# The second norm's weight and shift moved from token rows to the experts' transposed rows, and the first weight splits moved behind the first gather

## The chip, the core and the metric

The kernel runs on one core of a Trainium2 chip. The metric is the device time of one execution in microseconds (us); a lower time is better. The core has a matrix engine (PE, with PEld for its weight loads), a vector engine (DVE), an activation engine (ACT), GpSimd (POOL in the rows) and SyncE (SP), which issues most DMAs. Each takes its own instructions in order and waits for others by semaphores.

## What is computed

A whole model over 1024 tokens of width 1024 in float32: a first block of two attention layers, and a second block of a Fourier and window attention mix with a mixture of experts. The change concerns the end of the second block:

```python
h2 = rmsnorm(x, norm_ffn_g[l]) * (1.0 + sc2) + sh2
x = x + g2 * expert_choice_moe(h2, w_router[l], w_gate[l], w_up[l], w_down[l])

def expert_choice_moe(h, w_router, w_gate, w_up, w_down):
    cap = CAPACITY_FACTOR * S // N_EXPERTS          # 128 tokens
    aff = jax.nn.softmax(jnp.einsum('bsd,de->bse', h, w_router).astype(jnp.float32), axis=-1)
    g, idx = lax.top_k(aff.transpose(0, 2, 1), cap)
    xin = jax.vmap(lambda hb, ib: hb[ib])(h, idx)
    a = jnp.einsum('becd,edf->becf', xin, w_gate)
    u = jnp.einsum('becd,edf->becf', xin, w_up)
    y = jnp.einsum('becf,efd->becd', jax.nn.silu(a) * u, w_down)
    y = y * g[..., None].astype(y.dtype)
    ...
```

Here `sc2`, `sh2` and `g2` are three of the six parts of `mod`, a product of the conditioning vector with `w_ada`. The 16 experts each take the 128 tokens with the highest affinity, and their results, weighted, are added onto the rows of `x`.

## The kernel before

**Tiles and precision.** Tokens are worked in 8 tiles of 128 rows. A float32 product is made of three PE products of a high and a low half (`_h`, `_l`): ACT casts a tile to its high half, DVE subtracts that from the tile to get the low half (`kk.split`, lines 134 and 135), and lines 139 to 141 multiply high by high, low by high and high by low.

**The modulation vector.** Early in the program six rows of `mod` are made in pieces of 1x256 on one partition (lines 1297 to 1303) and written to memory as `mod_d`. Its row 3 holds weight times (1 + scale) of the second norm, row 4 its shift, row 5 the gate `g2`.

**The second norm (`norm2`, lines 2007 to 2044), once per tile, called by `out_phase` as the tiles of the second block's output projection come out.** PE transposes the tile, ACT and DVE split it, and PE makes 16 products with the router's weights, into which the weight of the norm is already multiplied (`wg`); the shift enters as a row sum `sw`. ACT reads the logits `rlg`, PE transposes them back (`prt`, line 2021), and the softmax follows in small instructions: `rz`, `rmx`, `rnm` on DVE, the exponential `rex` on ACT with its sum read by an accumulator instruction, then `rrc` (line 2032), `aff` (line 2033) and a spread copy `rep` (line 2050) on DVE, which PE transposes as `pa` (line 2052) so that ACT and DVE can keep it as `affr` and `affb`. The inverse root of the mean square, `r`, is made by ACT's sum of squares (`sqj`) and Newton steps on DVE over 128x1 (lines 148 to 163: `rsv`, `rsy`, `rsq`). Beside this the normed row `h2` is made in spare weight buffers (named `mraw`): for the first six tiles DVE multiplies `x` by `r` and by the broadcast weight `gB` in one instruction (line 2042); for the last two ACT multiplies by `r` (line 2039) and GpSimd by `gB` (line 2040); for all eight GpSimd adds the broadcast shift `sB` (line 2043). SP writes it to `h_d` (line 2044).

**The experts (`moe`, line 1619).** At its start the gate row is broadcast to `g2b` and halved by DVE (line 1624). Then 192 weight loads of 1 MB are issued by SP as buffers come free (line 1649; `mraw` and `xraw` are these buffers). Three quarters of each weight matrix are split, half a load at a time, into a ring of five slots, `ring_h` by ACT (line 1664) and `ring_l` by DVE (line 1665); the first five of these low halves are given to GpSimd (`spare`), behind the last `affr` copy. One quarter of the matrix is multiplied unsplit (line 1792). A threshold search of ten rounds follows (lines 1680 to 1688): a compare with a count over 128x1024 on DVE, `mok`, a PE product, and two small DVE instructions. Then come prefix counts and slots, and for each expert one-hot rows `oh`, a PE product `psel`, the row list `idx` and the gate (lines 1752 to 1759), and GpSimd's gather of 128 rows from `h_d` into `xg` (line 1756).

**The gathered rows.** `transposed(x, xT, g)` is called twice per expert for its rows: PE transposes four blocks of 128 columns into a PSUM tile `ptx`. For g = 0 ACT and DVE split blocks 2 and 3 (`xT_h`, `xT_l`), and ACT copies blocks 0 and 1 whole to `xTf` (line 1776), the operand of the unsplit products; for g = 1 all four blocks are split. The same function serves the hidden activations.

**What sets the order.** Up to the experts a scheduler places the recorded instructions on each engine by its own costs; `moe` itself, from its step functions on, is in the order in which it is written (`manual_schedule`): the first expert's one-hots, gather and transposes, then for each expert the products of gate, up and down, into whose parts the next expert's gather and transposes are put (parts 6 and 7 of the down product).

Of the kernel before, what the change touches and what calls it, by code (L numbers as in the profile page):

```python
# [11 lines left out]
F32 = mybir.dt.float32  # L12
# [1249 lines left out]
def ada_rows(kk, ps, a, mod_d):  # L1262
# [28 lines left out]
    def total(s, z, dst, gname, ap_):  # L1291
# [7 lines left out]
        nc.vector.tensor_tensor(x[0:1, :], pm[0:1, :H], b, op=ALU.add)  # L1299
        if gname:  # L1300
            nc.sync.dma_start(b, a[gname][:, z * H:z * H + H])
            nc.vector.scalar_tensor_tensor(x[0:1, :], x[0:1, :], 1.0, b, op0=ALU.add, op1=ALU.mult)
# [297 lines left out]
def moe_consts(kk, pool, a):  # L1600
# [3 lines left out]
    src = {"grp": a["c_grp"], "jsh": a["c_jsh"], "tri": a["c_tri"], "pidx": a["c_pidx"], "iota": a["c_iota"].to_broadcast([P, P])}  # L1604
    for nme, n, dt in (("grp", P, F32), ("jsh", 11, I32), ("tri", P, F16), ("pidx", 2 * NT, F32), ("iota", P, F16), ("one", P, F16)):
        c[nme] = pool.tile([P, n], dt, name="mc_" + nme)
# [9 lines left out]
def moe(kk, ctx, ax, a, con, aff, h2_d, acc_d, mod_d, raws, after):  # L1616

    nc = kk.nc
# [5 lines left out]
    nc.vector.tensor_scalar(g2, g2, 0.5, None, op0=ALU.mult)  # L1624
# [35 lines left out]
    def split_ahead(n, spare=False):  # L1660
        while count["split"] < min(n, len(splits)):
# [3 lines left out]
            (nc.gpsimd if spare else nc.vector).tensor_tensor(w.lo, raw_of(i), w.hi.bitcast(F32), op=ALU.subtract)  # L1665
# [4 lines left out]
    with kk.tc.issue_after(con["last"]):  # L1670
        split_ahead(RING, True)
# [97 lines left out]
    def transposed(x, xT, g):  # L1769

        pt = ps.tile([P, 4, P], F32, name=kk.nm("ptx"), **ptag)
        for j in range(4):
            nc.tensor.transpose(pt[:, j, :], x[:, (4 * g + j) * P:(4 * g + j + 1) * P], kk.ident)
        if g == 0:
            kk.split(xT.hl[:, 0:2, :], pt[:, 2:4])
            nc.scalar.copy(xT.full, pt[:, 0:2])
# [35 lines left out]
    def x_part(e, g):  # L1812
        if e < NE:
            if g == 0:
                xT[e] = Operand("xT")
            transposed(sel[e][2], xT[e], g)

    step_one_hots(0)
    step_gather(0)
    for g in range(2):  # L1820
        x_part(0, g)
# [27 lines left out]
def tile_model(ctx: ExitStack, tc: tile.TileContext, a: dict, out: bass.AP, part=None):  # L1849
# [116 lines left out]
    with kk.pool(name="c2", bufs=1) as op:  # L1966
        def setup():


            g2 = bcast(kk, op, mod_d[3:4, :], D, "gB3")  # L1970
            s2 = bcast(kk, op, mod_d[4:5, :], D, "sB3")
# [3 lines left out]
            cols = op.tile([P, 2, NK], F32, name="gscol")  # L1975
# [13 lines left out]
            return g2, s2, wr, sw, fold  # L1989
# [17 lines left out]
        def norm2(t, x):  # L2007
            if t == 0:
                router.extend(setup())
            g2, s2, wr, sw, fold = router  # L2010
# [27 lines left out]
            if t > 5:  # L2038
                nc.scalar.activation(h2, x, AF.Copy, scale=r)
                nc.gpsimd.tensor_tensor(h2, h2, g2, op=ALU.mult)  # L2040
            else:
                nc.vector.scalar_tensor_tensor(h2, x, r, g2, op0=ALU.mult, op1=ALU.mult)
            nc.gpsimd.tensor_tensor(h2, h2, s2, op=ALU.add)
# [105 lines left out]
```

## Time and profile before

| | |
|---|---|
| time, median of 3 runs (lowest to highest) | 2636.35 us (2634.61 to 2644.07) |
| profiled execution: time, span | 2629.75 us, 2628.0 us |
| busy: PE, DVE, ACT, POOL | 2338.4, 1841.4, 1265.6, 510.7 us |
| share of the span: PE, DVE, ACT, POOL | 89%, 70%, 48%, 19% |
| chain that ended last: PE, DMA, DVE, POOL, ACT | 56%, 17%, 12%, 5%, 3% |
| moved by DMA | 527.98 MB, 201 GB/s in the mean |

The span is the stretch from the first to the last instruction that the profiler saw; the execution's own time is a little longer. Matmul ends are modelled, so a busy PE is not necessarily at its peak. A row of the timeline gives the start, the duration, the engine, the line of the kernel, what it writes and reads with the shapes, and in brackets the idle time of that engine before it and what ended that.

### The profile page before, as it was taken

The numbers are of one execution on the slowest core, as the hardware profiler recorded it, in microseconds if no ns is written. First come the engines' busy times: TensorE is split into PE (matmuls) and PEld (weight loads), VectorE is DVE, ScalarE is ACT, GpSimd is POOL, SyncE is SP. The second block draws the span as 40 slices with busy tenths as digits, with TensorE's granted clock in tenths as the row PEclk, the third lists the DMA queues.
The fourth block names the chain that finished last, engine by engine and source line by source line (L and its number), as shares of the span: only waits on it lengthen the run. The fifth ranks groups of instructions, "written<-read, shape, count | busy, mean of one in ns | idle before, by whom it ended". The sixth has DMA issues, their size and how long they took to land.

```text
span 2628.0 us, 40820 instructions
## 1 busy us (share of the span) xinstructions
PE 2338.4 (89%) x14412; PEld 1844.6 (70%) x14412; DVE 1841.4 (70%) x4592; ACT 1265.6 (48%) x2423; POOL 510.7 (19%) x661
## 2 busy tenths in 40 slices
PE   7988978787978878899989969989974999999998
PEld 7866756665867866788767758877863776777676
DVE  4459989787866355366776576777676777777775
ACT  4344575465643243255654343355332555555554
POOL 0000027577770013100000031011022101110110
PEclk9999988897999899999999989999986999999999
DMA  4443376855656226854765452544564999999993
GB/s 129 134 124 100 113 206 167 208 162 183 185 167 205 77 98 255 255 145 124 191 186 157 135 195 68 140 119 157 197 264 168 359 369 357 356 374 367 356 357 128
DMA packets 298653, 527.98 MB, mean 201 GB/s; under 512 B 44086, under 2 KB 187598, under 8 KB 298448
## 3 DMA queue, kind: packets, MB, share of 16 engines
q1 hardware_dynamic: 282320, 467.69, 54.5%
q0 software_dynamic: 16128, 57.68, 6.9%
q8 instruction: 114, 1.87, 0.3%
q14 instruction: 91, 0.75, 0.1%
HBM read 409.37 MB, written 115.65 MB: 200 GB/s over the span
## 4 chain that ended last, share of the span: by engine, by line
PE 56%; DMA 17%; DVE 12%; POOL 5%; issue 5%; ACT 3%; SPq 2%; POOLq 0%; DVEq 0%; ACTq 0%
PE sb L139 6%; PE sb L140 6%; PE sb L141 6%; PE sb L288 4%; DMA adw<-w_ada 4%; PE ptp L335 3%; DVE tkj L392 3%; PE w_gate L1792 2%; POOL adw L1283 2%; PE w_up L1792 2%; PE w_down L1792 2%; PE w_gate L139 2%; PE w_gate L141 2%; PE w_gate L140 2%; PE w_up L139 2%
## 5 line engine op out<-in xcount | busy, mean ns | idle before, releaser
L337 DVE TENSOR_TENSOR pTl<-ptp,pTh 128x512 f16<-128x512 f32 (+2 forms) x316 | 201.1, 649 | 39.7 <-ACT pTh L336 39.1
L336 ACT CAST pTh<-ptp 128x512 f16<-128x512 f32 (+2 forms) x316 | 165.7, 556 | 121.7 <-PE ptp L335 115.2
L1665 DVE TENSOR_TENSOR ring_l<-mraw,ring_h 128x1024 fp32r<-128x1024 f32 x147 | 178.1, 1222 | 58.8 <-ACT ring_h L1664 56.6
L1665 DVE TENSOR_TENSOR ring_l<-xraw,ring_h 128x1024 fp32r<-128x1024 f32 x136 | 164.7, 1223 | 49.2 <-ACT ring_h L1664 47.9
L335 PE MATMUL ptp<-ident,e 128*128 128x128 f32 x1184 | 184.0, 286 | 9.7 <-DVE e L668 5.8
L1664 ACT CAST ring_h<-mraw 128x1024 fp32r<-128x1024 f32 x152 | 156.2, 1049 | 70.0 <-PE w_gate L141 33.8
L1664 ACT CAST ring_h<-xraw 128x1024 fp32r<-128x1024 f32 x136 | 140.5, 1049 | 58.7 <-PE w_gate L141 26.6
L335 PEld LDWEIGHTS ptp<-ident,e 128*128 128x128 f32 x1184 | 134.8, 145 | 24.4 <-DVE e L668 8.1
L347 PEld LDWEIGHTS <-pTl 128*128 128x128 f16 x1184 | 108.6, 100 | 41.5 <-DVE pTl L337 15.5
L887 ACT ACTIVATE e<-e,nmx 128x1024 f32<-128x1024 f32 (+7 forms) x128 | 98.5, 771 | 74.7 <-DVE nmx L886 39.2
L1232 ACT ACTIVATE e<-e,nmx 128x1024 f32<-128x1024 f32 (+7 forms) x128 | 98.4, 771 | 74.6 <-DVE nmx L1230 74.3
L345 PEld LDWEIGHTS <-pTh 128*128 128x128 f16 x1184 | 110.4, 100 | 32.6 <-issue 19.1
L1283 POOL TENSOR_SCALAR adw<-adw,ada_s 128x256 f32<-128x256 f32 x192 | 107.8, 574 | 93.8 <-DMA adw<-w_ada 93.6
L1756 POOL DMA_INDIRECT xg<-h_d,idx x16 | 23.8, 1485 | 506.3 <-DVE gate L1759 465.3
L346 PEld LDWEIGHTS <-pTh 128*128 128x128 f16 x1184 | 110.4, 100 | 13.3 <-issue 12.3
L1924 POOL TENSOR_TENSOR x<-x,gBf 128x1024 f32<-128x1024 f32 x8 | 19.5, 2434 | 468.2 <-DMA mxt<-mix_d 442.4
L139 PE MATMUL sb<-hold_h,w_h 128*128 128x512 f32 x272 | 108.2, 398 | 1.5 <-DVE tkatkc L389 1.5
L140 PE MATMUL sb<-hold_l,w_h 128*128 128x512 f32 x272 | 107.6, 395 | 0.0
L288 PE MATMUL sb<-hold_l,q 128*128 128x512 f32 (+3 forms) x384 | 104.7, 361 | 3.0 <-DMA q<-qr 3.0
L141 PE MATMUL sb<-hold_h,w_l 128*128 128x512 f32 x272 | 107.3, 396 | 0.0
L345 PE MATMUL pv<-vh,pTh 128*128 128x64 f16 (+1 forms) x608 | 85.6, 205 | 18.5 <-ACT oa L676 10.3
L312 DVE CUSTOM_DVE_ANT_0 e<-sb,hide 128x512 f32<-128x512 f32 (+3 forms) x128 | 74.5, 583 | 37.4 <-PE sb L288 22.1
(596 smaller groups left out, 7656.0 us busy)
## 6 DMA issues: line engine op xcount, KB each, us to landing
mraw<-w_up SPq DMA_DIRECT2D x35, 1024.0 KB
mraw<-w_gate SPq DMA_DIRECT2D x34, 1024.0 KB
mraw<-w_down SPq DMA_DIRECT2D x33, 1024.0 KB
xraw<-w_down SPq DMA_DIRECT2D x30, 1024.0 KB
xraw<-w_gate SPq DMA_DIRECT2D x30, 1024.0 KB
xraw<-w_up SPq DMA_DIRECT2D x29, 1024.0 KB
adw<-w_ada SPq DMA_DIRECT2D x96, 256.0 KB
xh_d<-hx SPq DMA_DIRECT2D x48, 256.0 KB
```

What stands on the lines that cost most here:

```text
L139: mm(out, a.hi, b.hi, start=start, stop=False)
L140: mm(out, a.hi, b.lo, start=False, stop=False)
L141: mm(out, a.lo, b.hi, start=False, stop=stop)
L288: mm(sc, a, b[:, k0:k0 + n], start=i == 0, stop=i == len(pairs) - 1)
L335: nc.tensor.transpose(pt[:, j, :], p[:, (g + j) * P:(g + j + 1) * P], kk.ident)
L336: nc.scalar.copy(hi[:, g:g + w, :], pt[:, :w, :])
L337: nc.vector.tensor_tensor(lo[:, g:g + w, :], pt[:, :w, :], hi[:, g:g + w, :], op=ALU.subtract)
L345: mm(out, hi[:, j, :], v1(off + j), start=j == 0, stop=False)
L1283: nc.gpsimd.tensor_scalar(w[:, k], w[:, k], ca[:, q + k:q + k + 1], 1.0, op0=ALU.mult, op1=ALU.mult)
L1664: nc.scalar.copy(w.hi, raw_of(i))
L1665: (nc.gpsimd if spare else nc.vector).tensor_tensor(w.lo, raw_of(i), w.hi.bitcast(F32), op=ALU.subtract)
L1792: nc.tensor.matmul(acc[n], xT.full[:, j, :], raw_of(i)[:, j], start=j == 0, stop=False)
```

## The change

1. `norm2` makes `h2` as `x` times `r` alone, by one ACT instruction per tile (eight in place of two). DVE's six products of line 2042, GpSimd's two products and eight additions, and the two broadcast loads `gB` and `sB` go.
2. Weight and shift, as columns (one value per partition and block, `mc_gs`), are applied by ACT after the transposition, in `transposed`: eight instructions over 128x128 per expert with a scale and a bias per partition. Blocks 0 and 1 go straight to `xTf`; the others go to a new tile `xfull`, of which there is one, and the split reads that in place of PSUM. The columns were `gscol` in a pool of the norm, and now live in the constants' pool.
3. The halving of the gate moves from `g2b` to the four 1x256 pieces of row 5 of `mod`, where they are made.
4. The first five ring splits are written behind the first gather, and their low halves are DVE's.

```diff
@@ the modulation's pieces @@
         nc.vector.tensor_tensor(x[0:1, :], pm[0:1, :H], b, op=ALU.add)
+        if dst == 5:
+            nc.vector.tensor_scalar(x[0:1, :], x[0:1, :], 0.5, None, op0=ALU.mult)
@@ moe_consts @@
+    c["gs"] = pool.tile([P, 2, NK], F32, name="mc_gs")
@@ moe @@
     g2 = bcast(kk, mx, mod_d[5:6, :], D, "g2b")
-    nc.vector.tensor_scalar(g2, g2, 0.5, None, op0=ALU.mult)
...
-    def split_ahead(n, spare=False):
+    def split_ahead(n):
...
-            (nc.gpsimd if spare else nc.vector).tensor_tensor(w.lo, raw_of(i), w.hi.bitcast(F32), op=ALU.subtract)
+            nc.vector.tensor_tensor(w.lo, raw_of(i), w.hi.bitcast(F32), op=ALU.subtract)
...
     load_ahead()
-    with kk.tc.issue_after(con["last"]):
-        split_ahead(RING, True)
...
-    def transposed(x, xT, g):
+    def transposed(x, xT, g, gs=None):
...
+        if gs is not None:
+            f = xp.tile([P, 4, P], F32, tag="xfull", name=kk.nm("xfull"), bufs=1)
+            for j in range(4):
+                k = 4 * g + j
+                nc.scalar.activation(xT.full[:, j] if k < 2 else f[:, j], pt[:, j], AF.Identity, bias=gs[:, 1, k:k + 1], scale=gs[:, 0, k:k + 1])
+            pt = f
+        elif g == 0:
+            nc.scalar.copy(xT.full, pt[:, 0:2])
         if g == 0:
             kk.split(xT.hl[:, 0:2, :], pt[:, 2:4])
-            nc.scalar.copy(xT.full, pt[:, 0:2])
...
-            transposed(sel[e][2], xT[e], g)
+            transposed(sel[e][2], xT[e], g, con["gs"])
...
     step_gather(0)
+    split_ahead(RING)
@@ the norm's set-up and norm2 @@
-            g2 = bcast(kk, op, mod_d[3:4, :], D, "gB3")
-            s2 = bcast(kk, op, mod_d[4:5, :], D, "sB3")
-            cols = op.tile([P, 2, NK], F32, name="gscol")
+            cols = con["gs"]
...
-            if t > 5:
-                nc.scalar.activation(h2, x, AF.Copy, scale=r)
-                nc.gpsimd.tensor_tensor(h2, h2, g2, op=ALU.mult)
-            else:
-                nc.vector.scalar_tensor_tensor(h2, x, r, g2, op0=ALU.mult, op1=ALU.mult)
-            nc.gpsimd.tensor_tensor(h2, h2, s2, op=ALU.add)
+            nc.scalar.activation(h2, x, AF.Copy, scale=r)
             nc.sync.dma_start(h2_d[rows, :], h2)
```

GpSimd from the norm's last tiles to the gathers, before (`mraw` are the `h2` rows, `ring_l` the low halves of the ring):

```order
L2043 TENSOR_TENSOR mraw_22691<-mraw_22691,sB_4626_22794 128x1024 x2
L2040 TENSOR_TENSOR mraw_22692<-mraw_22692,gB_4625_22792 128x1024
L2043 TENSOR_TENSOR mraw_22692<-mraw_22692,sB_4626_22794 128x1024
L2040 TENSOR_TENSOR mraw_22692<-mraw_22692,gB_4625_22792 128x1024
L2043 TENSOR_TENSOR mraw_22692<-mraw_22692,sB_4626_22794 128x1024
L1665 TENSOR_TENSOR ring_l<-mraw_22686,ring_h 128x1024
L1665 TENSOR_TENSOR ring_l<-mraw_22687,ring_h 128x1024
L1665 TENSOR_TENSOR ring_l<-mraw_22688,ring_h 128x1024
L1665 TENSOR_TENSOR ring_l<-mraw_22686,ring_h 128x1024
L1665 TENSOR_TENSOR ring_l<-mraw_22687,ring_h 128x1024
L1756 DMA xg_23899<-h_d,idx_23897 128x1024
L1756 DMA xg_23964<-h_d,idx_23962 128x1024
```

The same engine after: behind the constant `mc_one` the gathers follow directly.

```order
L906 TENSOR_TENSOR woraw_21950<-woraw_21950,g1b_21622 128x1024
L906 TENSOR_TENSOR woraw_22212<-woraw_22212,g1b_21622 128x1024
L906 TENSOR_TENSOR woraw_22472<-woraw_22472,g1b_21622 128x1024
L1614 MEMSET mc_one 128x128
L1757 DMA xg_23878<-h_d,idx_23876 128x1024
L1757 DMA xg_23962<-h_d,idx_23960 128x1024
L1757 DMA xg_24198<-h_d,idx_24196 128x1024
```

Twelve rows, fifteen instructions, are gone between the constant and the first gather. DVE around the first gather, before (`gate` ends the choice of the first expert's rows, `xT_l` are the splits of its transposed rows, `oh` the next expert's one-hots):

```order
L1754 SCALAR_TENSOR_TENSOR idx_23897<-sel_23895 128x1
L1758 TENSOR_TENSOR gate_23901<-sel_23895 128x1
L1759 TENSOR_TENSOR gate_23901<-gate_23901,sel_23895 128x1
L135 TENSOR_TENSOR xT_l<-ptx_23907,xT_h 128x256
L135 TENSOR_TENSOR xT_l<-ptx_23915,xT_h 128x512
L1745 TENSOR_SCALAR oh<-mc_iota,slot 128x128 x8
L1665 TENSOR_TENSOR ring_l<-mraw_22688,ring_h 128x1024
L1752 COPY sel_23960<-psel_23951 128x5
```

The same place after:

```order
L1755 SCALAR_TENSOR_TENSOR idx_23876<-sel_23874 128x1
L1759 TENSOR_TENSOR gate_23880<-sel_23874 128x1
L1760 TENSOR_TENSOR gate_23880<-gate_23880,sel_23874 128x1
L1668 TENSOR_TENSOR ring_l<-mraw_22691,ring_h 128x1024
L1668 TENSOR_TENSOR ring_l<-mraw_22692,ring_h 128x1024
L1668 TENSOR_TENSOR ring_l<-mraw_22693,ring_h 128x1024
L1668 TENSOR_TENSOR ring_l<-mraw_22691,ring_h 128x1024
L1668 TENSOR_TENSOR ring_l<-mraw_22692,ring_h 128x1024
L135 TENSOR_TENSOR xT_l<-xfull_23901,xT_h 128x256
L135 TENSOR_TENSOR xT_l<-xfull_23913,xT_h 128x512
L1746 TENSOR_SCALAR oh<-mc_iota,slot 128x128 x8
L1668 TENSOR_TENSOR ring_l<-mraw_22693,ring_h 128x1024
```

Five `ring_l` rows now stand between the gate and the first `xT_l`, and `xT_l` reads `xfull`, not PSUM. ACT at the boundary of the second and third expert, before:

```order
L1664 CAST ring_h<-xraw_23691 128x1024
L134 CAST xT_h<-ptx_24387 128x256
L1776 COPY xTf_24384<-ptx_24387 128x256
L1664 CAST ring_h<-xraw_23692 128x1024
L134 CAST xT_h<-ptx_24403 128x512
L1664 CAST ring_h<-xraw_23690 128x1024
L1664 CAST ring_h<-xraw_23691 128x1024
L1664 CAST ring_h<-xraw_23692 128x1024
```

The same place after:

```order
L1667 CAST ring_h<-xraw_23680 128x1024
L1779 ACTIVATE xTf_24391<-ptx_24394,mc_gs 128x128 x2
L1779 ACTIVATE xfull_24399<-ptx_24394,mc_gs 128x128 x2
L134 CAST xT_h<-xfull_24399 128x256
L1667 CAST ring_h<-xraw_23681 128x1024
L1779 ACTIVATE xfull_24419<-ptx_24414,mc_gs 128x128 x4
L134 CAST xT_h<-xfull_24419 128x512
L1667 CAST ring_h<-xraw_23679 128x1024
L1667 CAST ring_h<-xraw_23680 128x1024
```

Eight pieces stand where `xTf` was one copy, two to `xTf`, two to `xfull` for the first group's split and four to `xfull` for the second's, and the casts read `xfull`; one `ring_h` cast still stands between the two groups. On PE the scheduler's order changes in two further places: in the second layer of the first block twelve `poh` products stand some 25 rows earlier, and at the end of `out_phase` all of the last products of tile 7 stand ahead of the logits and transposes of the last tiles.

## Rows read from the trace of the kernel before

**Rows 1.** Windows: busy time (instructions) of each engine, granted clock, DMA share.

```profile
1878.00:1946.00 68.00, 65.86 (x408) 53.95 (x405) 47.20 (x123) 22.29 (x54) 14.43 (x7) 0.97 0.81 295
1946.00:1971.00 25.00, 11.43 (x78) 8.54 (x76) 18.04 (x52) 9.57 (x26) 9.78 (x4) 0.66 0.54 192
2055.00:2092.00 37.00, 37.00 (x155) 26.06 (x154) 28.96 (x40) 21.10 (x27) 4.14 (x2) 1.00 0.95 353
```

**Rows 2.** Timeline, tail of the norm: start us, duration, engine, line, operation [idle before].

```profile
1949.94 2.34 POOL L2040 TENSOR_TENSOR mraw<-mraw,gB 128x1024 f32<-128x1024 f32 x1 [6.60 <-ACT mraw L2039]
...
1949.97 0.18 ACT L2030 ACTIVATION_READ_ACCUMULATOR rex<-rz,rnm 128x1 f32 x1
...
1950.19 2.64 DVE L1624 TENSOR_SCALAR g2b<-g2b 128x1024 f32<-128x1024 f32 x1 [1.18 <-DMA g2b<-mod_d]
...
1952.36 2.66 POOL L2043 TENSOR_TENSOR mraw<-mraw,sB 128x1024 f32<-128x1024 f32 x1
...
1952.93 2.11 DVE L155 SCALAR_TENSOR_TENSOR rsq<-rsy,rsv 128x1 f32<-128x1 f32 x1
...
1955.95 0.48 PE L2052 MATMUL pa<-ident,rep 128*128 128x128 f32 x1 [5.20 <-DVE rep L2050]
...
1957.85 2.34 POOL L2040 TENSOR_TENSOR mraw<-mraw,gB 128x1024 f32<-128x1024 f32 x1 [2.83 <-ACT mraw L2039]
...
1957.87 0.19 ACT L2030 ACTIVATION_READ_ACCUMULATOR rex<-rz,rnm 128x1 f32 x1
...
1958.29 1.93 DVE L2033 TENSOR_SCALAR aff<-rex,rrc 128x16 f32<-128x16 f32 x1
...
1960.54 0.47 PE L2052 MATMUL pa<-ident,rep 128*128 128x128 f32 x1 [1.63 <-DVE rep L2050]
...
1968.32 0.19 ACT L2030 ACTIVATION_READ_ACCUMULATOR rex<-rz,rnm 128x1 f32 x1
...
1969.29 0.47 PE L2052 MATMUL pa<-ident,rep 128*128 128x128 f32 x1 [1.62 <-DVE rep L2050]
```

**Rows 3.** Timeline, threshold search; last row: all `mok` instructions, ns min/median/max.

```profile
1970.79 1.27 DVE L1680 TENSOR_SCALAR_CACHE_REDUCE oh<-affb,mc_jsh 128x1024 bf16<-128x1024 bf16 x1
...
1971.08 11.57 POOL L1665 TENSOR_TENSOR ring_l<-mraw,ring_h 128x1024 fp32r<-128x1024 f32 x5 [8.38 <-ACT ring_h L1664]
...
1983.81 1.28 DVE L1680 TENSOR_SCALAR_CACHE_REDUCE oh<-affb,mcand 128x1024 bf16<-128x1024 bf16 x1
...
1999.60 1.28 DVE L1680 TENSOR_SCALAR_CACHE_REDUCE oh<-affr,mcand 128x1024 bf16<-128x1024 f32 x1
...
L1682 DVE TENSOR_SCALAR mok<-mcnt x10: 168/170/1360, 1972.1 to 2000.9; 128x2 f32<-128x2 f32 x10
```

**Rows 4.** Timeline, from the first gather's index to the first expert.

```profile
2009.44 0.16 DVE L1759 TENSOR_TENSOR gate<-gate,sel 128x1 f32<-128x1 f32 x1
...
2014.47 1.97 PE L1773 MATMUL ptx<-ident,xg 128*128 128x128 f32 x8 [5.54 <-DMA xg<-h_d,idx]
...
2015.63 0.37 ACT L134 CAST xT_h<-ptx 128x256 fp32r<-128x256 f32 x1 [40.84 <-PE ptx L1773]
...
2016.49 0.37 ACT L1776 COPY xTf<-ptx 128x256 f32<-128x256 f32 x1 [0.49 <-DVE xT_l L135]
```

**Rows 5.** One line's gathers (ns min/median/max); the loop's `ring_l` group (busy, mean ns).

```profile
L1756 POOL DMA_INDIRECT xg<-h_d,idx x16: 1056/1518/1522, 2010.2 to 2548.8; - x16
...
L1665 DVE TENSOR_TENSOR ring_l<-mraw,ring_h 128x1024 fp32r<-128x1024 f32 x147 | 178.1, 1222 | 58.8 <-ACT ring_h L1664 56.6
```

**Rows 6.** All ACT copies over 128x128 at the norm's end (ns min/median/max).

```profile
L2053 ACT COPY affr<-pa x8: 250/266/266, 1916.1 to 1969.8; 128x128 f32<-128x128 f32 x8
```

**Rows 7.** Timeline, boundary of the second and third expert.

```profile
2094.17 0.68 DVE L135 TENSOR_TENSOR xT_l<-ptx,xT_h 128x512 fp32r<-128x512 f32 x1
...
2096.64 0.39 PE L139 MATMUL w_gate<-ring_h,xT_h 128*128 128x512 f32 x1
```

**Rows 8.** DVE instructions over 1x256 where the modulation is made (ns min/median/max).

```profile
L1302 DVE SCALAR_TENSOR_TENSOR adx<-adx,mb x8: 406/410/414, 1231.3 to 1411.7; 1x256 f32<-1x256 f32 x8
```

More of the change, by code (lines that the diff above doesn't have):

```diff
@@ L1988, in setup @@
                 load_con()
-            return g2, s2, wr, sw, fold
+            return wr, sw, fold
         router, loads = [], []
@@ L2009, in norm2 @@
                 router.extend(setup())
-            g2, s2, wr, sw, fold = router
+            wr, sw, fold = router
             rows = slice(t * P, (t + 1) * P)
```

## The prediction

> **What bounds the kernel now.** I read the windows first, then the timeline of the two stretches in which PE has holes, then the groups by line for prices. The windows [rows 1] split the end of the program into a part that PE fills and a part that it does not. From 1878 to 1946 us PE is busy 65.86 of 68 us, and in the expert loop 37.00 of 37 us: there, only PE's own work counts, and what ACT, DVE and GpSimd do is hidden as long as it is not late. From 1946 to 1971 us PE is busy 11.43 of 25 us at a granted clock of 0.66, so partly at the lower of its two levels (1.2 and 2.4 GHz). That stretch, and the one behind it up to the first expert, whose first operand is ready at 2016.86 [rows 4], are chains of small instructions on DVE, ACT and PE, and there every delay is paid in full. All that the change can gain lies in these 70 us; all that it can lose lies at the expert boundaries.
>
> In the tail of the norm the chain runs from ACT's softmax exponential through three small DVE instructions to PE's transpose `pa`, and PE's later work queues behind that transpose. Undisturbed it is short: at the last tile the accumulator is read by 1968.51 (1968.32 + 0.19) and `pa` starts at 1969.29, 0.78 us later. Two tiles earlier the same step takes from 1950.15 (1949.97 + 0.18) to 1955.95, that is 5.80 us, and one tile earlier from 1958.06 to 1960.54, 2.48 us [rows 2]. The rows in between name the cause: DVE first spends 2.64 us on the halving of `g2b`, beside GpSimd's product, and then an `rsq` over 128x1 takes 2.11 us and the division `aff` 1.93 us, each ending when GpSimd's product or addition over 128x1024 ends.
>
> The threshold search shows the same. Its ten rounds start at 1970.79, and the fourth at 1983.81, so the first three take 13.02 us; the tenth starts at 1999.60, so the six rounds from the fourth to the ninth take 15.79 us, 2.63 us each. The slow ones run beside the five `ring_l` subtractions of GpSimd, 11.57 us in all, and their `mok` over 128x2 takes up to 1360 ns against a median of 170 [rows 3].
>
> **The change, part by part.** *Search.* The five subtractions leave GpSimd, and nothing else is queued there until the gather. Three rounds of 2.63 us in place of 13.02 us give 13.02 - 7.89 = **-5.1 us**.
>
> *Tail of the norm.* GpSimd's eight additions and two products go, and so does the `g2b` halving. Both long steps should fall to the 0.78 us of the last tile: 5.80 - 0.78 = 5.02 and 2.48 - 0.78 = 1.70, together **-6.7 us**. What is late next is ACT: the exponentials follow its 128x1024 copies there, but those were already ACT's for the last two tiles, so the time of the exponentials does not move. Bounds: -5.1 if PE's order of the tail (the last products of tile 7 now stand ahead of the logits and transposes) costs what a further small wait costs here, twice 0.8 us; -8.2 if PE also keeps its clock: it did 11.43 us of work in that stretch at 0.66, which at the 0.97 of the stretch before would be 7.8, and I allow 1.5 of the 3.6 us for work on the path. I take -6.7, since no row shows how the clock would go.
>
> *The six tiles before.* There DVE loses six products and ACT gains six copies. PE fills this stretch, and ACT is busy 22.29 of its 68 us [rows 1], so both count nothing; without that cover a copy would cost about what DVE's 128x1024 subtraction does, 1.22 us [rows 5], six times.
>
> *Before the first expert.* The five subtractions, now DVE's, stand right behind the gate, whose second addition ends at 2009.60 [rows 4]. At 1.22 us each [rows 5] they end at 2015.7. Nothing on DVE is wanted earlier: PE gets the gathered rows at 2014.47, and the first split of the transposed rows could follow only after ACT's casts. So they cost nothing, and the cover is the wait for the gather. The gather's issue ran 1056 ns here, where DVE was idle, and 1518 ns in the median of all sixteen, mostly beside DVE's subtractions [rows 5]: +0.46 us. Against it, PE's first product now waits for two ACT pieces in place of a cast, DVE's split and a copy: before, ACT began at 2015.63 and the copy `xTf` ended at 2016.86 [rows 4]; two pieces of 128x128 at 266 ns [rows 6] end 0.53 us after that start, 0.70 earlier. Together **-0.2 us**; bounds -0.7 (no slower gather) and +1.1 (a gather that also lands 0.6 later with none of the rest changed, or a split that waits once more).
>
> *The expert loop.* For each expert ACT gets eight pieces of 266 ns, 2.13 us, and loses the `xTf` copy of 0.37: +1.76 us. DVE's work there is the same. New is a wait: there is one `xfull` buffer, so the first piece of the second group waits for DVE's split of the first, and behind it on ACT stand that group's cast and the next `ring_h` casts, for which DVE's `ring_l` and then PE wait. The trace gives the room: the second group's split ends at 2094.85 (2094.17 + 0.68), and PE comes to that part of the operand at 2096.64 [rows 7], 1.8 us later. The added 1.76 us does not use it up, because ACT's order now puts only one `ring_h` ahead of the second group, as before, and part of the added work falls into the time in which ACT stood idle for DVE's first split (0.49 us at the first expert [rows 4]). I take **0**, with the thinnest cover of all the terms.
>
> *The rest.* The halving becomes four DVE instructions over 1x256, far ahead, in a stage of PE's products; one such takes at most 414 ns [rows 8], so 0 to +1.6 us, and I take 0, since what they feed is read only in the experts. The two broadcast loads that vanish were long done. The column tile `mc_gs` is loaded earlier, off the path. Twelve `poh` products in the first model's second layer move forward by some 25 places among PE's rows; no row prices that. The nearest is the second tail step above, where one instruction that came late cost the rows behind it 1.70 us, so 1.7 us to either side, 0 taken.
>
> **The sum.** -5.1 - 6.7 - 0.2 = -12.0 us. The profiled execution took 2629.75 us (its span is 2628.0), and so would take 2617.75; that is 0.9954 of it, and 0.9954 of the median of 2636.35 is **2624 us**. A measurement of this kernel can tell about 0.5% from no change, 13.2 us here: the forecast lies just on the near side of it.
>
> **The rivals.** *The boundary stalls (slower).* The new wait on `xfull` lengthens the chain at each of the fifteen later experts. It decides from the point at which the chain is more than the 1.8 us late [rows 7]. If DVE has two `ring_l` of 1.22 us queued ahead of the first split, the second group comes 1.76 + 2.44 = 4.2 us later, PE waits 2.4 us at each boundary, and 15 x 2.4 = 36 us against 12 gained gives +24: 2660. With 0.8 us each the gain is just eaten, 2636. For it: DVE's queue at the boundary is full. Against it: PE has no idle time there, and ACT was waiting for DVE rather than the reverse. Chance 0.06, 0.04 of it above the 0.5%.
>
> *The gather is held behind the subtractions.* If GpSimd's descriptor work for the gather waits for DVE's five subtractions, the rows land as late as those end: 2015.7 - 2009.60 = 6.1 us later, less the part that the issue overlaps; I price it at +5.8, so the sum is -6.2: 2630. For it: DVE and GpSimd clearly hold each other up in [rows 2, 3]. Against it: in the loop, beside the same kind of subtraction, the longest issue of sixteen is 1522 ns [rows 5]. Chance 0.08. The Trainium skill, "SBUF — State Buffer", section "Who interferes with whom", has a rule that speaks for this rival: a DVE instruction with both inputs in SBUF contends with a GpSimd instruction that reads SBUF, and the loser blocks for the whole of the other instruction. By that rule the sum would be this rival's if reading the index list counts as such a read; the loop's rows show at most half a microsecond, so I give the row more weight.
>
> *The tail keeps its length.* Another wait takes the place of GpSimd's, for instance ACT's 128x1024 copies ahead of each exponential, and PE's rows in their new order wait for them. Then only the search and the start remain, -5.3: 2631. For it: those copies sit in the chain already. Against it: the exponentials were done at 1950.15 and 1958.06 while PE waited for what came after them [rows 2]. Chance 0.11.
>
> *The change doesn't do what it says* (GpSimd's work is gone but the small DVE instructions stay slow): 2636, chance 0.02.
>
> **How the numbers follow.** My forecast keeps 0.73. Its own terms reach from -5.1 - 5.1 + 1.1 + 1.6 + 1.7 = -5.8 with all going wrong to -5.1 - 8.2 - 0.7 - 1.7 = -15.7 with all going right; beyond that only the scatter of the runs, which were 2634.61 to 2644.07. Taking in the gather and the tail rivals (2630, 2631) on the high side, and half of what PE's clock could still give on the low side, the range is 2614 to 2633. Faster by over 0.5% means below 2623.2; the forecast is 1 us above that, and the two terms that I took at 0 or left out, clock and order, can as well help: 0.36. Slower by over 0.5% is the boundary rival alone: 0.04. Between them lie 0.60.
>
> **What would show it.** Right: search rounds all 2.6 us from the first; exponential to `pa` 0.8 us at each of the last tiles; `g2b` loaded without a DVE instruction behind it; five `ring_l` between gate and first split; PE 37 of 37 us in the loop. Wrong: PE idle before the third part of `w_gate` with ACT's piece or DVE's split as releaser (boundary); the gather's issue several microseconds long (gather); `pa` or the logits waiting for ACT (tail).

## The result and the profile after

The changed kernel took 2622.12 us in the median of 9 runs (2611.31 to 2628.68), beside 2641.2 us (2632.25 to 2644.3, 9 runs) for the kernel before: a ratio of 0.9939 with an interval of 0.9922 to 0.9956, by that ratio about 16 us less (the two medians lie 19 apart). The forecast was a gain of 12 us and a time of 2624 us, and the bound of 0.5% was passed, which had been given a chance of 0.36.

Where it came from can be read only stretch by stretch. The two profiled executions are just 2.5 us apart in span (2628.0 and 2625.5), because the one of the kernel before had been quick far ahead of the change: its first logits product of the second norm starts at 1902.9 us, that of the changed kernel at 1913.8. Of the experiments below, the two with the old norm come to that product at 1908.2 and 1910.6, the eight with the new one between 1911.7 and 1916.9. That scatter lies ahead of the changed norm and has the sign opposite to the gain; where it comes from no run shows. So I take stretches that start at that product. These are the rows of before that mark them, beside the first compare at 1970.79 [rows 3]; they give the count, ns min/median/max, first and last start:

```profile
L2017 PE MATMUL prt<-xT_h,wr x64: 220/223/316, 1902.9 to 1966.3; 128*32 128x128 f32 x64
...
L1693 DVE COPY my<-mcand x1: 226/226/226, 2002.2 to 2002.2; 128x128 f32<-128x128 f32 x1
...
L1792 PE MATMUL w_gate<-mraw,xTf x56: 591/592/1222, 2016.9 to 2589.1; 128*128 128x512 f32 x56
```

The same marks after, with the ten `mok` of the search:

```profile
L2024 PE MATMUL prt<-xT_h,wr x64: 218/223/316, 1913.8 to 1969.6; 128*32 128x128 f32 x64
...
L1681 DVE TENSOR_SCALAR_CACHE_REDUCE oh<-affb,mc_jsh x1: 1277/1277/1277, 1974.0 to 1974.0; 128x1024 bf16<-128x1024 bf16 x1
...
L1683 DVE TENSOR_SCALAR mok<-mcnt x10: 169/169/171, 1975.3 to 1999.0; 128x2 f32<-128x2 f32 x10
...
L1694 DVE COPY my<-mcand x1: 226/226/226, 2000.3 to 2000.3; 128x128 f32<-128x128 f32 x1
...
L1800 PE MATMUL w_gate<-mraw,xTf x56: 592/592/1174, 2014.8 to 2587.1; 128*128 128x512 f32 x56
```

From them, and from the same lines of each experiment:

| stretch (us) | before | after | changed by |
|---|---|---|---|
| norm: first logits product to first compare | 67.9 | 60.2 | -7.7 |
| search: first compare to the result's copy | 31.4 | 26.3 | -5.1 |
| start: that copy to the first expert's product | 14.7 | 14.5 | -0.2 |
| loop: that product to the end of the span | 611.1 | 610.7 | -0.4 |

That is -13.4 us, inside the interval of the runs (11.6 to 20.6 less). A stretch scatters too: the experiment that leaves the norm as it was (part 4 alone, below) has 69.3 us for it where the kernel before has 67.9. Engines and chain of the page after:

```profile
PE 2343.4 (89%) x14412; PEld 1850.1 (70%) x14412; DVE 1828.1 (70%) x4594; ACT 1314.7 (50%) x2541; POOL 476.0 (18%) x646
...
PE 56%; DMA 17%; DVE 9%; POOL 6%; issue 5%; ACT 3%; SPq 1%; POOLq 0%; DVEq 0%; ACTq 0%
```

GpSimd lost 35 us and ACT gained 49; the chain has less DVE (9% where 12% stood) and PE's 56% as before. The tail of the norm after, in the timeline (start, duration, engine, line, operation):

```profile
1959.94 0.22 DVE L155 SCALAR_TENSOR_TENSOR rsq<-rsy,rsv 128x1 f32<-128x1 f32 x1
...
1960.02 0.19 ACT L2037 ACTIVATION_READ_ACCUMULATOR rex<-rz,rnm 128x1 f32 x1
...
1960.99 0.33 PE L2054 MATMUL pa<-ident,rep 128*128 128x128 f32 x1 [0.20 <-DVE rep L2052]
...
1962.77 0.19 ACT L2037 ACTIVATION_READ_ACCUMULATOR rex<-rz,rnm 128x1 f32 x1
...
1963.74 0.48 PE L2054 MATMUL pa<-ident,rep 128*128 128x128 f32 x1
...
1971.55 0.19 ACT L2037 ACTIVATION_READ_ACCUMULATOR rex<-rz,rnm 128x1 f32 x1
...
1972.52 0.48 PE L2054 MATMUL pa<-ident,rep 128*128 128x128 f32 x1 [1.50 <-DVE rep L2052]
```

From the end of the accumulator's read to `pa` it is 0.78 us at each of the three tiles of [rows 2] (1960.21 to 1960.99, 1962.96 to 1963.74, 1971.74 to 1972.52), where these had 5.80, 2.48 and 0.78; and the `rsq` of 2.11 us is one of 0.22. The first of these tiles is the fifth of eight. From the read of its accumulator to that of the last tile it is 11.53 us (1960.02 to 1971.55) where it was 18.35 (1949.97 to 1968.32), so 6.82 of the 7.7 us lie in the tail, and 0.85 between the first logits product and the fifth tile. The search after, its first two compares:

```profile
1974.02 1.28 DVE L1681 TENSOR_SCALAR_CACHE_REDUCE oh<-affb,mc_jsh 128x1024 bf16<-128x1024 bf16 x1
...
1976.65 1.28 DVE L1681 TENSOR_SCALAR_CACHE_REDUCE oh<-affb,mcand 128x1024 bf16<-128x1024 bf16 x1
```

The second round starts 2.63 us after the first, and no `mok` takes over 171 ns (above; [rows 3]: 1360). From the gate to the first expert:

```profile
2007.55 0.16 DVE L1760 TENSOR_TENSOR gate<-gate,sel 128x1 f32<-128x1 f32 x1
2007.63 5.76 DVE L1668 TENSOR_TENSOR ring_l<-mraw,ring_h 128x1024 fp32r<-128x1024 f32 x5
2008.38 1.40 POOL L1757 DMA_INDIRECT xg<-h_d,idx  x1 [118.23 <-DVE gate L1760]
...
2013.07 1.97 PE L1774 MATMUL ptx<-ident,xg 128*128 128x128 f32 x8 [6.02 <-DMA xg<-h_d,idx]
2014.27 0.81 ACT L1779 ACTIVATE xTf<-ptx,mc_gs 128x128 f32<-128x128 f32 x2 [36.25 <-issue]
...
2014.83 1.65 PE L1800 MATMUL w_gate<-mraw,xTf 128*128 128x512 f32 x2
```

The five subtractions end at 2013.4, ahead of ACT's first piece; the gather's issue takes 1.40 us, and the two pieces of `xTf` 0.81 us together ([rows 4]: a cast, a split and a copy). PE's first product starts at 2014.83, before the second piece ends (2015.08), so it waits for one piece only. A boundary in the loop, the same as in [rows 7]:

```profile
2091.23 1.50 ACT L1779 ACTIVATE xfull<-ptx,mc_gs 128x128 f32<-128x128 f32 x4
...
2092.76 0.62 ACT L134 CAST xT_h<-xfull 128x512 fp32r<-128x512 f32 x1
...
2093.41 0.69 DVE L135 TENSOR_TENSOR xT_l<-xfull,xT_h 128x512 fp32r<-128x512 f32 x1 [0.83 <-ACT xT_h L134]
...
2094.88 0.39 PE L139 MATMUL w_gate<-ring_h,xT_h 128*128 128x512 f32 x1
...
2095.12 0.19 PEld L141 LDWEIGHTS w_gate<-ring_h,xT_l 128*128 128x128 f32 x1
```

The second group's split ends at 2094.10, and PE comes to that group at 2094.88: 0.78 us are left of the 1.8 that the same reading gave before. But the product at 2094.88 reads the cast `xT_h`, which ended at 2093.38; the split `xT_l` is wanted first by the weight load at 2095.12. Measured there the room is 1.02 us, and in the kernel before, where that load starts at 2096.88, it is 2.03. PE still has no hole there (window of the loop, columns as in [rows 1]):

```profile
2055.00:2092.00 37.00, 37.00 (x156) 26.38 (x155) 28.58 (x41) 23.75 (x33) 4.12 (x2) 1.00 0.91 337
```

### The profile page after: what moved, and what is told of

Its sections match the earlier page's. It is cut to its first block, busy times and chain, and to the rows that moved or that the text cites. A ratio compares the mean times of both kernels' runs of the same rounds, so it can differ in the third digit from the quotient of the medians.

```text
span 2625.5 us, 40884 instructions
## 1 busy us (share of the span) xinstructions
PE 2343.4 (89%) x14412; PEld 1850.1 (70%) x14412; DVE 1828.1 (70%) x4594; ACT 1314.7 (50%) x2541; POOL 476.0 (18%) x646
## 4 chain that ended last, share of the span: by engine, by line
PE 56%; DMA 17%; DVE 9%; POOL 6%; issue 5%; ACT 3%; SPq 1%; POOLq 0%; DVEq 0%; ACTq 0%
PE sb L139 6%; PE sb L140 6%; PE sb L141 6%; DMA adw<-w_ada 5%; PE sb L288 4%; DVE tkj L392 3%; PE ptp L335 3%; POOL adw L1283 2%; PE w_down L1800 2%; PE w_up L1800 2%; PE w_gate L1800 2%; PE w_up L139 2%; PE w_gate L139 2%; PE w_up L141 2%; PE w_up L140 2%
## 5 line engine op out<-in xcount | busy, mean ns | idle before, releaser
L1668 DVE TENSOR_TENSOR ring_l<-mraw,ring_h 128x1024 fp32r<-128x1024 f32 x152 | 183.8, 1223 | 33.6 <-ACT ring_h L1667 31.4
```

Of the source, the lines that this page charges most:

```text
L1668: nc.vector.tensor_tensor(w.lo, raw_of(i), w.hi.bitcast(F32), op=ALU.subtract)
```

## The experiments

Each gives the stretches of the table above; time ratios stand where several runs were timed, and the others are one profiled execution each.

**Part 4 alone on the kernel before.** Subtractions on DVE behind the gather, nothing else.

```diff
-    with kk.tc.issue_after(con["last"]):
-        split_ahead(RING, True)
...
     step_gather(0)
+    split_ahead(RING)
```

> The kernel before with part 4 of the change alone: the first five ring subtractions on DVE behind the first gather. Theory (GpSimd's work holds up DVE's small instructions): the search's ten rounds fall from 31.44 us to 26.3, the tail of the norm keeps its 5.80 and 2.48 us from exponential to pa, and the way from the search's end to the first expert stays near 14.7 us; the time falls by about 5 us, ratio 0.998. Rival (the search's slow rounds come from ACT's casts of the same pieces, which stay where they were): the search keeps 31 us and nothing changes.

Norm 69.3, search 26.3, start 15.2, loop 611.3 us; ratio 0.9982 (0.9966 to 0.9998). The search fell by 5.1 us although ACT's casts of the same pieces stayed where they were (4.83 us, from 0.83 ahead of the first compare, in both kernels), so the rival falls. The start grew by 0.5, and its gather shows why:

```profile
2011.83 1.40 POOL L1754 DMA_INDIRECT xg<-h_d,idx  x1 [42.51 <-DVE gate L1757]
```

Its issue takes 1.40 us beside DVE's subtractions.

**The changed kernel without part 4.** The subtractions on GpSimd again, as in the kernel before.

```diff
-    step_gather(0)
-    split_ahead(RING)
+    step_gather(0)
...
+    with kk.tc.issue_after(con["last"]):
+        split_ahead(RING, True)
```

> The changed kernel with part 4 undone: the five subtractions on GpSimd again, during the search. Theory: the search is back at 31.4 us, the norm's stretch from its first logits product to the search keeps the changed kernel's 60.2 us (67.9 before), so the time lies about 8 us under the kernel before, ratio 0.997. Rival (the tail is short because the whole schedule moved, not because GpSimd is idle): the norm's stretch is between 60 and 68 us although GpSimd does nothing in it.

Norm 60.4, search 31.4, start 14.3, loop 610.6 us; ratio 0.9956 (0.9941 to 0.9971). The two parts add up: 0.0018 and 0.0044 below one give 0.9938, and both together measured 0.9939. GpSimd's rows in it, the subtractions and the first gather:

```profile
1977.56 11.55 POOL L1668 TENSOR_TENSOR ring_l<-mraw,ring_h 128x1024 fp32r<-128x1024 f32 x5 [84.00 <-ACT ring_h L1667]
...
2016.66 1.05 POOL L1759 DMA_INDIRECT xg<-h_d,idx  x1 [27.55 <-issue]
```

The gather beside an idle DVE takes 1.05 us again. The norm keeps its short form, so it does not hang on part 4.

**Part 3 alone on the kernel before.** The halving where the gate is made; GpSimd's products and additions stay.

```diff
+        if dst == 5:
+            nc.vector.tensor_scalar(x[0:1, :], x[0:1, :], 0.5, None, op0=ALU.mult)
...
-    nc.vector.tensor_scalar(g2, g2, 0.5, None, op0=ALU.mult)
```

> The kernel before with part 3 alone: the gate is halved where it is made, so DVE's 2.64 us over g2b is gone, and GpSimd's products and additions stay. Theory (both matter, GpSimd more): the small instructions behind it still meet GpSimd's product or addition, so the first tail step falls from 5.80 to about 3 us and the second stays at 2.5 us; the norm's stretch falls from 67.9 to about 65 us. Rival (the halving alone made the tail long): both steps fall to about 0.8 us and the stretch to 61 us. Other rival (the halving lay in GpSimd's shadow): no change, 68 us.

Norm 67.1, search 31.4, start 14.8, loop 611.3 us: only 0.8 less, nearest to the rival that had it in GpSimd's shadow. That 0.8 is less than the norm's scatter, but from the fifth tile's accumulator read to the last tile's it is 17.62 us, where the two kernels with the old tail have 18.35 and 18.40, so a gain of 0.7 in the tail stands out. The first step did fall to 2.49 us, as the theory had it, and the second stayed at 2.48; the time came back elsewhere. The tail's small DVE instructions show what came in its place:

```profile
1957.97 1.95 DVE L2034 TENSOR_SCALAR aff<-rex,rrc 128x16 f32<-128x16 f32 x1
...
1960.44 1.96 DVE L163 SCALAR_TENSOR_TENSOR rsy<-rsy,rsy 128x1 f32<-128x1 f32 x1
...
1964.15 1.93 DVE L2034 TENSOR_SCALAR aff<-rex,rrc 128x16 f32<-128x16 f32 x1
```

Three instructions of 0.15 to 0.23 us are held for some 1.95 each, where before it was the halving and two of them; behind the `rsy` stand ACT's copy and the next exponential.

**The changed kernel without part 3.** DVE halves `g2b` again, with GpSimd idle.

```diff
-        if dst == 5:
-            nc.vector.tensor_scalar(x[0:1, :], x[0:1, :], 0.5, None, op0=ALU.mult)
...
+    nc.vector.tensor_scalar(g2, g2, 0.5, None, op0=ALU.mult)
```

> The changed kernel with part 3 undone: DVE halves g2b again, but GpSimd is idle. Theory (its 2.64 us were long because GpSimd's product ran beside it): it takes about 1.2 us or less, the exponential-to-pa step at that tile is 1 to 2.5 us in place of 0.8, and the norm's stretch is 60 to 62 us. Rival (the halving by itself costs 2.64 us and its DMA wait): 63 us or more.

Norm 63.5, search 26.4, start 14.6, loop 610.9 us: 3.3 more than the changed kernel, over what the theory gave. Its row:

```profile
1959.14 0.69 DVE L1626 TENSOR_SCALAR g2b<-g2b 128x1024 f32<-128x1024 f32 x1 [1.16 <-DMA g2b<-mod_d]
```

The halving itself takes 0.69 us, not 2.64, as the theory has it; but DVE first stands 1.16 us for the load of `g2b`, with the split of the next tile's transposes and the small instructions queued behind. Those 1.85 us are on the path: counted from the first logits product, the fifth tile's accumulator is read 1.84 us later. Of the other 1.5, 1.4 lie between the last two exponentials. There the last tile's sixteen logits products take 1.92 us at a granted clock of 0.50 (1.2 GHz), in the changed kernel 1.19 at 1.00 (2.4 GHz). PE's eight transposes ahead of them also took 1.92 us, 1.72 in the changed kernel, so some 0.9 of the 1.5 go with PE's clock. The step from exponential to `pa` at that tile is 0.99 us, as expected; the stretch is over the expected 60 to 62. Part 3 is worth 0.8 us with GpSimd's work in place and 3.3 without it: the gain of the tail belongs to both together and cannot be divided.

**The cover taken away.** The subtractions written ahead of the first gather.

```diff
-    step_gather(0)
-    split_ahead(RING)
+    split_ahead(RING)
+    step_gather(0)
```

> The changed kernel with the five ring subtractions written ahead of the first gather, behind the first one-hots, so that the wait for the gathered rows no longer covers them. Theory (they are free only through that cover): the way from the search's end to the first expert grows from 14.5 us by about 5.8 us to 20.3, less what PE's selection product overlaps, so 18.5 to 20.5; the gather's issue, now beside an idle DVE, falls from 1.40 us to 1.06. Rival (the subtractions cost the gather as much as they would cost alone, by holding up its issue and landing): the way stays at 14.5 to 16 us.

Norm 60.3, search 26.3, start 19.6, loop 610.7 us; ratio 0.9959 (0.9944 to 0.9975). The start is 5.1 us longer:

```profile
2005.92 5.76 DVE L1668 TENSOR_TENSOR ring_l<-mraw,ring_h 128x1024 fp32r<-128x1024 f32 x5
...
2012.86 1.06 POOL L1757 DMA_INDIRECT xg<-h_d,idx  x1 [124.73 <-DVE gate L1760]
...
2017.32 1.97 PE L1774 MATMUL ptx<-ident,xg 128*128 128x128 f32 x8 [11.08 <-DMA xg<-h_d,idx]
```

The subtractions' 5.76 us stand ahead of the gather, less the 0.34 us that its issue gains and what PE's selection product overlaps. Behind the gather they cost only what its issue and landing lose beside them, 0.3 to 0.5 us; one place earlier they cost almost their length.

**A GpSimd that only writes.** Five memsets of 128x1024 in the changed kernel.

```diff
+    with kk.tc.issue_after(con["last"]):
+        for w in ring:
+            nc.gpsimd.memset(w.lo.bitcast(F32), 0.0)
```

> The changed kernel with five GpSimd memsets over 128x1024 float32 put where the subtractions stood, at the start of the search (they fill the ring's low halves, which DVE writes later). They write and read nothing. Theory A (any GpSimd instruction holds up DVE's small ones): the search's first rounds are slow again, the search is 28 to 31 us in place of 26.3. Theory B (only a GpSimd instruction that reads SBUF does): the search stays at 26.3 us.

The scheduler put the memsets not into the search but into the tail, so the search's 26.3 us say nothing; but the norm's stretch stayed at 59.9 us, and the tail holds the instructions in question (start 14.8, loop 610.8):

```profile
1953.20 4.92 POOL L1675 MEMSET ring_l<- 128x1024 f32 x5 [64.51 <-PE sb L141]
...
1956.87 0.15 DVE L163 SCALAR_TENSOR_TENSOR rsy<-rsy,rsy 128x1 f32<-128x1 f32 x1
...
1957.78 0.22 DVE L155 SCALAR_TENSOR_TENSOR rsq<-rsy,rsv 128x1 f32<-128x1 f32 x1
```

The memsets ran to 1958.12. `rsy` and `rsq` beside them took 0.15 and 0.22 us, the same as alone; beside GpSimd's addition `rsq` took 2.11 [rows 2]. So it is not GpSimd's being busy that holds these two. It is a narrow test: no `aff` and no `mok`, which the subtractions and products of GpSimd had held, fell beside a memset, and the two casts over 128x128 that did took 0.58 and 0.63 us, 0.35 and 0.40 in the changed kernel. The Trainium skill, "SBUF — State Buffer", section "Who interferes with whom", says that a DVE instruction with two SBUF inputs contends with a GpSimd instruction that reads SBUF, and not with one that only writes it. The pair of runs agrees with that for `rsq`, which reads two tiles.

**ACT's pieces doubled, and by how much the boundary gives way.** Three runs add pieces that write the same result a second time: eight per expert, two at the head (`k < 2`), four in the second group (`g == 1`).

```diff
                 nc.scalar.activation(xT.full[:, j] if k < 2 else f[:, j], pt[:, j], AF.Identity, bias=gs[:, 1, k:k + 1], scale=gs[:, 0, k:k + 1])
+                nc.scalar.activation(xT.full[:, j] if k < 2 else f[:, j], pt[:, j], AF.Identity, bias=gs[:, 1, k:k + 1], scale=gs[:, 0, k:k + 1])
```

> The changed kernel with each of ACT's pieces for the transposed rows done twice, the second time over the first. It doubles the cost whose room was in doubt. In the changed kernel's trace the second group's split at a boundary ends about 1.0 us before PE needs it, and eight more pieces at a pitch of 0.38 us put it some 3 us later. Theory (the room is 1 us and the rest is paid at each of fifteen boundaries): PE waits some 2 us at each boundary, the loop grows from 610.7 us by 20 to 35 us, and the time is 4 to 19 us over the kernel before (ratio 1.002 to 1.007). Rival (ACT's and DVE's order gives way, because ACT stands idle two fifths of the time): the loop stays within 3 us of 610.7.

> The changed kernel with only the two pieces for xTf done twice: ten pieces per expert in place of eight, the added two at the head of ACT's chain at each boundary. At the measured pitch of 0.38 to 0.42 us the second group's split comes 0.8 us later, and the changed kernel's trace leaves 1.0 us before PE needs it. Theory (the room at the boundary is about 1 us): PE does not wait, the loop stays at 610 to 612 us. Rival (every added piece is paid from the first): the loop grows by 10 us or more.

> The changed kernel with only the four pieces of the second group done twice: twelve pieces per expert. The second group's split comes 1.6 us later, 0.6 more than the room. Theory: PE waits about 0.6 us for the second group's cast or split at each of fifteen boundaries, so the loop grows by 9 us from 610.7, and by somewhat more if PE's clock falls behind a wait, up to 15. Rival (the cast ring_h and the rest behind it on ACT give way first, or PE's queue covers it): the loop stays within 3 us of 610.7.

| pieces per expert | 8 | 10 | 12 | 16 |
|---|---|---|---|---|
| loop, us | 610.7 | 611.4 | 625.8 | 664.8 |
| over the changed kernel, per boundary (15) | | 0.05 | 1.0 | 3.6 |

Ten pieces fit, twelve don't. With ten, the split at this boundary ends at 2097.84, 0.05 us ahead of the weight load that wants it (2097.89): the two pieces took up the 1.02 us of room. With twelve, the second group's cast starts 1.96 us later behind its first piece (3.49 us in place of 1.53), some 0.9 more than the room, and 1.0 per boundary is what the loop lost. The sixteen gave a ratio of 1.014 (1.0115 to 1.0166). Twelve came out at the upper end of what was expected, sixteen far above it. A boundary with twelve shows one reason:

```profile
2095.14 0.40 PE L141 MATMUL w_gate<-ring_h,xT_l 128*128 128x512 f32 x1
2095.21 0.62 ACT L134 CAST xT_h<-xfull 128x512 fp32r<-128x512 f32 x1
...
2095.89 0.50 PE L139 MATMUL w_gate<-ring_h,xT_h 128*128 128x512 f32 x1 [0.35 <-ACT xT_h L134]
...
2096.22 0.40 PE L140 MATMUL w_gate<-ring_l,xT_h 128*128 128x512 f32 x1
```

The row of waits would put 0.35 us here, but between the starts of two products that otherwise follow 0.23 apart lie 0.75, and the next gap is 0.33: the bracket is less than what is lost; ends of matmuls are modelled. The same holds for the sum of PE's waits over the loop (us in total, times, longest):

```profile
PE w_gate L139 <- ACT xT_h L134: 5.4, 15, 0.6
```

5.4 us stand there for the 15.1 that the loop grew. With sixteen, PE's waits in the loop; then windows (columns as in [rows 1]) of the whole loop of the changed kernel, of the whole loop with sixteen, and of a stretch behind a boundary with sixteen:

```profile
PE w_gate L139 <- ACT xT_h L134: 31.0, 16, 2.6
PE psel L1751 <- ACT xfull L1780: 4.5, 14, 0.3
```

```profile
2014.80:2625.00 610.20, 601.42 (x2482) 424.28 (x2480) 458.77 (x623) 383.88 (x522) 62.53 (x31) 1.00 0.90 332
...
2013.00:2677.00 664.00, 620.41 (x2480) 429.48 (x2480) 456.15 (x623) 439.67 (x649) 62.49 (x31) 0.98 0.82 305
...
2143.00:2153.00 10.00, 10.00 (x34) 7.26 (x34) 9.21 (x13) 6.82 (x9) 4.09 (x2) 0.85 0.45 127
```

These waits sum to 35.5 us of the 54 that the loop grew. The rest stands in PE's busy time, 620.41 us in place of 601.42 for the same products. Behind some waits the clock is granted at 0.85 in place of 1.00, so products at the lower level (1.2 in place of 2.4 GHz) stand among them; how much of these 19.0 us is that, and how much is the gap above, no run separates.

**The next thing that is late in the tail.** ACT's copies of the last two tiles behind the last `affr`.

```diff
+            if t > 5:
+                late_rows.append((h2, x, r, rows))
+                return
             nc.scalar.activation(h2, x, AF.Copy, scale=r)
...
         spread(NT - 1)
+        with kk.tc.issue_after(con["last"]):
+            for h2, x, r, rows in late_rows:
+                nc.scalar.activation(h2, x, AF.Copy, scale=r)
+                nc.sync.dma_start(h2_d[rows, :], h2)
```

> The changed kernel with ACT's copies of the last two tiles' h2 rows, and their writes to memory, moved behind the last affr copy, so that the softmax exponentials of these tiles no longer stand behind them (1.15 us each). Theory (ACT's copies are the next thing that is late in the tail): the norm's stretch falls from 60.2 by 1 to 2 us, the search and the rest keep their length, ratio to the kernel before 0.9933. Rival (the transposed tile's casts and PE's transposes are as late as the exponentials): no change, 60.2 us. Other rival (the later writes hold up SyncE's weight loads): the loop starts late or PE waits for weights.

Norm 58.6, search 26.3, start 14.5, loop 610.5 us; ratio 0.9936 (0.9916 to 0.9957). The tail of it:

```profile
1962.66 0.15 DVE L2034 TENSOR_SCALAR rnm<-rmx 128x1 f32<-128x1 f32 x1
...
1963.09 0.59 ACT L134 CAST xT_h<-pt 128x512 fp32r<-128x512 f32 x1 [0.38 <-PE pt L262]
1963.57 0.31 ACT L2037 ACTIVATE rex<-rz,rnm 128x16 f32<-128x16 f32 x1
...
1963.78 0.19 ACT L2037 ACTIVATION_READ_ACCUMULATOR rex<-rz,rnm 128x1 f32 x1
...
1965.99 0.28 PE L2057 MATMUL pa<-ident,rep 128*128 128x128 f32 x1
```

The exponential no longer waits for a copy, but the first transposes' cast has taken its place ahead of it, 0.59 us where the copy took 1.15; and the step to `pa` at this tile is 2.02 us (1963.97 to 1965.99) in place of 0.78, with a split of the transposed tile between `rrc` and `aff` on DVE. The stretch is 1.6 us shorter than the changed kernel's. In the time this can't be told from it: 0.9936 beside 0.9939.

## Why the prediction held, step by step

**Search, -5.1.** Measured -5.1, and shown by doing part 4 alone (-5.1) and undoing it (+5.1).

**Tail, -6.7 (bounds -5.1 and -8.2).** The two steps named fell exactly as worked out, to 0.78 us each, 6.72 together, and the tail as a whole by 6.82. (They are not the last tile's two neighbours, as the prediction counts them, but the fifth and sixth of eight; the seventh has a step of 0.87 us before and 0.78 after.) The stretch fell by 7.7; of the 1.0 over, 0.85 lie ahead of the fifth tile's accumulator read, where the prediction had put nothing and where the kernel before and part 4 alone, with the same norm, differ by 1.3; so it is not PE's clock in the tail, which the low bound had allowed for. A window of 25 us before the search shows the clock granted at 0.82 where it was 0.66 [rows 1], but the tail is shorter, so that window holds more of the full stretch ahead of it. PE's new order is in every run without GpSimd's work and was not tried alone; beside the two steps 0.1 us is left for it. My reading of the cause was half right: the halving's 2.64 us were GpSimd's doing for the most part (0.69 alone), yet without GpSimd its wait for the load is a cost of its own.

**Start, -0.2.** Measured -0.2, and by the two parts that were expected. From the gate's end to the transposes it is 5.36 us (2007.71 to 2013.07) where it was 4.87 [rows 4], +0.49 for +0.46. From the transposes to the first product it is 1.76 us where it was 2.45 (1.76 without part 4, 2.44 with part 4 alone), -0.69 for -0.70. The second agreement is luck: the prediction had PE wait for two pieces of 0.27 us, and PE waited for one of 0.45. The gather's price came from the loop's median; it met 1.40 us, not 1.52.

**Loop, 0.** Measured -0.4, nothing beside the spread of the experiments (610.5 to 611.4 with ten pieces or fewer). The diff also puts the whole copy of the hidden activations' blocks ahead of their split, which the list of the change leaves out; the loop shows nothing of it. But the price under the 0 was wrong: I took a piece from the copy `affr`, 266 ns [rows 6], and it takes 454 (the row below). In a run they overlap: two take 0.81 us and four 1.50, so the eight take 3.1 us per expert where I had 2.13:

```profile
L1779 ACT ACTIVATE xTf<-ptx,mc_gs x32: 448/454/458, 2014.3 to 2577.2; 128x128 f32<-128x128 f32 x32
```

The Trainium skill, "ScalarE: Activation LUTs", section "What ACT_TABLE_LOAD costs", says that each per-partition pointer operand adds about 93 ns to an activation of 186 ns and 0.833 ns per element; for two of them and 128 elements that is an estimate of 479 ns, near the 454 measured. A copy has neither operand, so its row was the wrong neighbour.

The room was misread the other way: 2.03 us where the prediction read 1.8, since PE's first product of that group reads only the cast. It fell to 1.02 us. So the 0 held, but with two errors under it that partly cancel; doubling the second group's pieces alone was already too much, and the rival of the stalling boundary was nearer than its chance of 0.06 says.

**The gather's rival** (held until the subtractions end, +5.8) did not come: +0.5. **The tail's rival** did not either, though ACT's copies are in fact the next thing there, worth 1.6 us.

**The sum.** -12.0 predicted, -13.4 by stretches, -16 by the runs, whose interval starts at 11.6. The mechanism and the terms held; the forecast lies near the small end of that interval. The 2.6 us between the last two stay open: measured from the first product of the same output projection, 1.1 us of them appear (88.9 us to the first compare before, 80.1 after), but ahead of that the profiled executions differ by up to 15 us, and not in the direction of the gain. The 0.5% was passed by the 1.0 us of the norm's stretch, ahead of the tail for the most part, that no term held, and by whatever those 2.6 us are.

## What to carry to other kernels

Look for small vector instructions on a serial chain that share their time with GpSimd instructions that read large SBUF tiles: here some instructions of 0.2 us became 1.4 to 2.1 us beside them, on both chains, and were short again without them. Work that must go to the vector engine is almost free where that engine waits for a transfer (5.8 us behind a gather, for 0.3 to 0.5), and it cost 5.1 us one place earlier. Before adding work to an engine that feeds a full PE, read the room at the tightest hand-over in the timeline, up to the instruction that reads the late operand, and price the instruction by its own form: a scale and a bias per partition took 454 ns where a plain copy of the same shape took 266.

## What the runs showed of the hardware

- ACT's Identity with a scale and a bias per partition on 128x128 from PSUM: 454 ns in the median, a plain copy of that shape 266 [rows 6].
- DVE's halving over 128x1024 in SBUF: 0.69 us with GpSimd idle, 2.64 beside GpSimd's product and addition [rows 2].
- GpSimd's memset of 128x1024 (4.92 us for five) did not hold an `rsq` (0.22 us) or an `rsy` (0.15); beside its additions of 2.4 to 2.7 us an `rsq` took 2.11 and an `rsy` 1.96, up to the addition's end.
- The gather's issue on GpSimd: 1.05 us beside an idle DVE, 1.40 beside DVE's subtractions.
- A wait of PE cost more than its row says: 1.0 us per boundary where the rows sum to 5.4 us over fifteen of them.
- PE's sixteen logits products of one tile: 1.19 us at a granted clock of 1.00, 1.92 at 0.50.
